# A hybrid decoder layer on one core: the FFN's down-projection by seven block products instead of eight, and its up-projection with the weights as the moving operand

## The chip, the cores and the metric

The kernel runs on one core of a Trainium2 chip. The metric is the device time in microseconds of one execution. Three executions of the kernel before took 1066.48, 1064.62 and 1064.70 us, median 1064.7.

The engines go by these names: PE is TensorE (matrix products), DVE is VectorE, ACT is ScalarE, POOL is GpSimd, SP issues most DMAs.

## The reference: what is computed

One layer over 256 tokens of width 2048, all in float32:

```python
h = rmsnorm(x, g_mix)
z = h @ w_in                       # conv, pooling and attention heads
x = x + concat(conv, pool, att) @ w_out
h = rmsnorm(x, g_ffn)
u = causal_dwconv(h @ w_up, ffn_conv_w) + ffn_conv_b      # width 3 over the tokens
gate, val = split(u, 2)
x = x + (silu(gate) * val) @ w_down
return rmsnorm(x, g_final)
```

`w_up` is 2048 x 11264 and `w_down` 5632 x 2048, so the FFN holds 92.3 and 46.1 of the 202 MB that are read. Each weight is read once and used for 256 tokens.

## The kernel before

**Products.** A float32 operand is split into two float32r parts, `hi` (a rounded copy) and `lo` (the rest), and a product is made of three: hi x hi, hi x lo, lo x hi. Every weight goes through `split_piece`: ACT writes `hi` (L129), DVE subtracts it from the raw tile to give `lo` (L130). The activations are split in the same way when they are made.

**The stream of weights.** All weight tiles, 1 MB each, form one list, `stream`. `next_tile` hands out the next split tile; before it does, it emits the loads up to three tiles ahead (L118, on SP's queue) and the splits up to two ahead. `raw`, `hi` and `lo` have three buffers each.

**The two forms of a product.** `mm_a` (L306, L309) keeps the weights as the stationary operand and streams the activations, 256 tokens of hi and of lo side by side: a matmul of 512 columns with the weight's `hi`, and one of 256 with its `lo`. Its result has channels in the partitions. `mm_b` (L338, L341, L344) keeps 128 tokens of the activation stationary and streams 512 columns of the weights, three matmuls of 512. Its result has tokens in the partitions.

**The FFN.** The up-projection goes by 22 units of 256 gate and 256 value channels, each in form a (`unit_a`). `up_finish` then takes each chunk of 128 channels out of PSUM: `gather` adds the main and the correction columns and multiplies by the row of the norm's factors (ACT L322, DVE L323, L324), ACT applies the last tap and the bias (L747), DVE the other two taps (L751), ACT the silu (L755). The gate times the value is split into `u` (L776 to L778). The units form groups of 8, 7, 5 and 2; `down` multiplies a finished group by `w_down` in form b and adds it to the residual `xt` (`add_in`, L706). It comes after the next group's first unit, that of the last but one group after all units. `down_last` takes the last group by column pieces, with the final norm between them.

**The order.** In the first part and in `down_last`, PE, DVE and ACT keep the program's order. Between them a planner orders each engine's instructions ahead of time, by their place in the program and its own estimate of when their inputs are ready; on the chip each engine then runs its list in that order. Activations lie in three buffers of 32 KB per partition (`apool`), and PSUM gives eight banks of 512 columns.

Of the kernel before, what the change touches and what calls it, by code (L numbers as in the profile page):

```python
# [24 lines left out]
def kernel(  # L25
# [45 lines left out]
    # Per-channel vectors, as columns of 128 channels, by transposing rows of 128.  # L71
# [20 lines left out]
    rows = lambda v: v.rearrange("(r c) -> r c", c=P)  # noqa: E731  # L92
# [10 lines left out]
    stream = []  # (source, nk, ncol, pieces)  # L103
# [4 lines left out]
    def load(i, between=None):  # L108
        src, nk, ncol, pieces = stream[i]
        raw = wpool.tile([P, nk, ncol], F32, tag="raw", name=f"raw_{i}")  # L110
# [23 lines left out]
    def split_tile(i):  # L134
        nk, pieces = stream[i][1], stream[i][3]
        step = nk // pieces
        for j in range(0, nk, step):
            split_piece(i, j, j + step)
        loaded.pop(i)
# [16 lines left out]
    n_units = NF // 2  # L156
    UNITS = [8, 7, n_units - 17, 2]  # sizes of FFN groups in units of 256 channels
# [20 lines left out]
    # The pool's weights: per pair of groups the three chunks' rows, in the columns of  # L178
    # the output chunks that they reach; wp_at[k] is the first of them.
# [17 lines left out]
    # Chunks of the mix in the order in which they come about.  # L197
# [10 lines left out]
    # A group's down-projection comes after the next group's first unit; that of the  # L208
    # last but one after all units.
    sched = []  # L210
    done = 0
    for gi, (a, n) in enumerate(group_of):
        upto = n_units if gi + 2 >= len(group_of) else a + n + 1
        for u in range(done, upto):
            sched.append(("up", u, [g for g, (b, m) in enumerate(group_of) if b <= u][-1]))
        done = upto
        sched.append(("down", gi, None))
    for what, a, b in sched:
        if what == "up" and a == 0:
            for h in (0, 1):  # L220
                plan_a(w_up, 0, (h,))
                plan_a(w_up, D_UP, (h,))
        elif what == "up":
            plan_a(w_up, a * 256)
            plan_a(w_up, D_UP + a * 256)
        else:
            a0, n = group_of[a]
            for n2 in range(2):
                plan_b(w_down, a0 * 2, n * 2, n2 * 1024, 1024, 2)

# [27 lines left out]
    def rstd_of(ssq, nm):  # L258
        """ssq [P, n] sums of squares -> 1 / sqrt(mean + eps), with a Newton step."""
# [14 lines left out]
    def row_of(r, nm):  # L274
        """[P, TB] per-token values -> the same row of S values in every partition."""
# [44 lines left out]
    def gather(ps, row, o, engine=nc.vector):  # L320
        """(main + corrections) * row -> o [P, S] in SBUF."""
        nc.scalar.activation(o, ps[:, S:], AF.Copy)  # L322
        nc.vector.tensor_tensor(o, ps[:, :S], o, op=ALU.add)  # L323
        engine.tensor_tensor(o, o, row, op=ALU.mult)  # L324
# [44 lines left out]
    # The order of the first instructions is that in which the data arrive.  # L369
# [66 lines left out]
    def split_into(o, src, n=S):  # L436
        """float32 [P, n] -> o, its two parts one after the other."""
# [50 lines left out]
    # 1 / (number of tokens averaged) for the first tokens  # L488
# [73 lines left out]
    # The sums run on GpSimd while the next unit's products do; the rest comes after.  # L562
    pending = []

    def pool_sums(ps, i):
# [3 lines left out]
        spans = []  # (first row, last row, group) of this chunk  # L569
# [17 lines left out]
    def pool_means():  # L587
        for i, v, spans, sums in pending:
# [11 lines left out]
            # The convolution's chunks of the mix are free until it comes.  # L600
# [122 lines left out]
    row_2 = None  # L723
    u_tiles = {}

    def up_matmul(u):
        if u:
            return [unit_a(h2T, f"g{u}"), unit_a(h2T, f"v{u}")]
        ps = [[bank(f"pu0_{w}_{mi}") for mi in range(2)] for w in range(2)]
        for h in range(2):  # L730
            for w in range(2):
                mm_a(ps[w], next_tile(), h2T, h * 8, 8, h == 0, h == 1)
                if h == 0 and w == 0:
                    transpose_in(xt, h2T, "g_ffn", range(8, 16), "x2")
        return ps

    def up_finish(ps, u, w):
        """main + corrections, norm, convolution and bias of one half of a unit."""
        outs = []
        for mi in range(2):  # L740
            m = w * NF + u * 2 + mi
            hp = spool.tile([P, S + 2], F32, tag="hpad", name=f"h_{u}_{w}_{mi}", bufs=HPAD)
            nc.gpsimd.memset(hp[:, :2], 0.0)
            gather(ps[mi], row_2, hp[:, 2:])
            t = spool.tile([P, S], F32, tag="w1k", name=f"t_{u}_{w}_{mi}", bufs=6)
            cw = [cvec("ffn_conv_w", j * 2 * NF + m) for j in range(3)]
            nc.scalar.activation(  # L747
                t, hp[:, 2:], AF.Identity, bias=cvec("ffn_conv_b", m), scale=cw[2]
            )
            for s in (1, 0):  # L750
                nc.vector.scalar_tensor_tensor(  # L751
                    t, hp[:, s : s + S], cw[s], t, op0=ALU.mult, op1=ALU.add
# [4 lines left out]
        return outs  # L757

    def up(u, gi):
        nonlocal row_2  # L760
        if gi not in u_tiles:
            u_tiles[gi] = apool.tile([P, 16, 2 * S], F32R, tag="act", name=f"u_{gi}")
        ut = u_tiles[gi]
        base = group_of[gi][0]
        if u == 0:
            ps_g, ps_v = up_matmul(0)
            row_2 = row_of(rstd_sum(ssq4, "x2"), "x2")
            gates = up_finish(ps_g, u, 0)
        else:
            ps_g = unit_a(h2T, f"g{u}")  # L770
            gates = up_finish(ps_g, u, 0)
            ps_v = unit_a(h2T, f"v{u}")
        vals = up_finish(ps_v, u, 1)
        for mi in range(2):
            c = (u - base) * 2 + mi
            nc.vector.tensor_tensor(gates[mi], gates[mi], vals[mi], op=ALU.mult)  # L776
            nc.scalar.activation(ut[:, c, :S], gates[mi], AF.Copy)
            nc.vector.tensor_tensor(  # L778
                ut[:, c, S:], gates[mi], ut[:, c, :S].bitcast(F32), op=ALU.subtract
            )  # L780

    def down(gi):
        ut = u_tiles[gi]
        nk = group_of[gi][1] * 2
        for n2 in range(2):
            ps = [[bank(f"pd_{gi}_{n2}_{tb}_{n}") for n in range(2)] for tb in range(TB)]
            for i in range(nk // 2):
                mm_b(ps, next_tile(), ut, (2 * i, 2 * i + 1), range(TB), i == 0, i == nk // 2 - 1)
            add_in(ps, n2 * 2, range(TB), f"d{gi}")

    # The last group goes by token blocks and column pieces, each followed by its share
    # of the final norm, so that little is left after the last product.
    def down_last(gi):
        ut = u_tiles[gi]
        nk = group_of[gi][1] * 2
# [31 lines left out]
        def partial(tb):  # L827
            """The mean square + eps, but for the last piece."""
# [4 lines left out]
        def rstd_last(tb):  # L833
            """-2 / sqrt(mean square + eps), with a Newton step."""
# [20 lines left out]
        with tc.manual_schedule(engines=IN_ORDER):  # L855
# [32 lines left out]
    for what, a, b in sched:  # L888
        if what == "up":
            up(a, b)  # L890
        elif a < len(group_of) - 1:
            down(a)
        else:
            down_last(a)
# [31 lines left out]
```

## Time and profile before

| | before |
|---|---|
| median of three runs | 1064.7 us |
| the profiled execution: its span | 1064.7 us |
| PE busy | 1054.7 us, 5632 matmuls |
| DVE busy | 703.6 us, 920 instructions |
| ACT busy | 529.0 us, 683 instructions |
| POOL busy | 43.1 us, 163 instructions |
| moved by DMA | 202.01 MB, mean 190 GB/s |

The span goes from the first to the last instruction; the profiled execution's own time is that span. A row of instruction groups gives the line, engine and operation, the output and inputs by their names in the program, the count, then busy time and the mean of one in ns, then the engine's idle time ahead of them and what ended it. "pd" is the down-projection's PSUM, "pa_g" and "pa_v" those of the gate and the value, "pl" that of the last group. Matmuls overlap, so the time of one row is longer than the step from one start to the next. In the view by stretches the columns are the stretch, its length, then PE, weight load, DVE, ACT and POOL busy time with counts, the clock that was granted to PE, and the DMAs' share and rate.

### The profile page before, as it was taken

The numbers are of one execution on the slowest core, as the hardware profiler recorded it, in microseconds if no ns is written. First come the engines' busy times: TensorE is split into PE (matmuls) and PEld (weight loads), VectorE is DVE, ScalarE is ACT, GpSimd is POOL, SyncE is SP. The second block draws the span as 40 slices with busy tenths as digits, with TensorE's granted clock in tenths as the row PEclk, the third lists the DMA queues.
The fourth block names the chain that finished last, engine by engine and source line by source line (L and its number), as shares of the span: only waits on it lengthen the run. The fifth ranks groups of instructions, "written<-read, shape, count | busy, mean of one in ns | idle before, by whom it ended". The sixth has DMA issues, their size and how long they took to land.

```text
span 1064.7 us, 14249 instructions
## 1 busy us (share of the span) xinstructions
PE 1054.7 (99%) x5632; PEld 907.2 (85%) x5632; DVE 703.6 (66%) x920; ACT 529.0 (50%) x683; POOL 43.1 (4%) x163
## 2 busy tenths in 40 slices
PE   9999999999999999999999999999999999999996
PEld 8888898888888888888888888888888888888885
DVE  5677786764556777777744467777754477777655
ACT  5965454443446655555533344554533345555343
POOL 0023500000000000000000000000000000000000
PEclk9999999999999999999999999999999999999998
DMA  9765465455555556555555555655555555654552
GB/s 316 243 224 172 143 206 189 161 195 183 186 185 174 184 196 198 188 181 185 198 198 198 196 171 187 198 185 175 195 198 197 191 174 190 198 177 178 198 198 80
DMA packets 147342, 202.01 MB, mean 190 GB/s; under 512 B 3619, under 2 KB 125771, under 8 KB 147147
## 3 DMA queue, kind: packets, MB, share of 16 engines
q1 hardware_dynamic: 147242, 201.09, 55.8%
q8 instruction: 44, 0.72, 0.3%
q14 instruction: 24, 0.19, 0.0%
q10 hardware_dynamic: 32, 0.01, 0.0%
HBM read 198.99 MB, written 2.10 MB: 189 GB/s over the span
## 4 chain that ended last, share of the span: by engine, by line
PE 98%; DVE 1%; ACT 0%; issue 0%; DVEq 0%
PE pa_v L306 15%; PE pa_g L306 15%; PE pa_g L309 7%; PE pa_v L309 7%; PE pd L338 7%; PE pd L344 7%; PE pd L341 7%; PE po L338 3%; PE po L341 3%; PE po L344 3%; PE pa_cc L306 2%; PE pa_cx L306 2%; PE pa_cb L306 2%; PE pa_pv L306 2%; PE pk L395 2%; PE pa_q L306 1%
## 5 line engine op out<-in xcount | busy, mean ns | idle before, releaser
L130 DVE TENSOR_TENSOR lo<-raw,hi 128x2048 fp32r<-128x2048 f32 (+2 forms) x196 | 425.5, 2172 | 271.6 <-ACT hi L129 270.6
L129 ACT ACTIVATE hi<-raw 128x2048 fp32r<-128x2048 f32 (+2 forms) x196 | 355.9, 1818 | 255.8 <-PE pd L344 98.4
L306 PE MATMUL pa_v<-h2T,hi 128*128 128x512 f32 x672 | 236.7, 396 | 0.0
L306 PE MATMUL pa_g<-h2T,hi 128*128 128x512 f32 x672 | 236.7, 396 | 0.0
L309 PE MATMUL pa_g<-h2T,lo 128*128 128x256 f32 x672 | 188.5, 281 | 0.0
L309 PE MATMUL pa_v<-h2T,lo 128*128 128x256 f32 x672 | 188.5, 281 | 0.0
L306 PEld LDWEIGHTS pa_v<-h2T,hi 128*128 128x128 f32 x672 | 126.0, 188 | 30.0
L306 PEld LDWEIGHTS pa_g<-h2T,hi 128*128 128x128 f32 x672 | 126.0, 188 | 30.0
L309 PEld LDWEIGHTS pa_g<-h2T,lo 128*128 128x128 f32 x672 | 127.0, 189 | 0.1
L309 PEld LDWEIGHTS pa_v<-h2T,lo 128*128 128x128 f32 x672 | 127.0, 189 | 0.0
L338 PE MATMUL pd<-hi,u 128*128 128x512 f32 x320 | 98.6, 389 | 0.0
L341 PE MATMUL pd<-lo,u 128*128 128x512 f32 x320 | 98.5, 389 | 0.0
L344 PE MATMUL pd<-hi,u 128*128 128x512 f32 x320 | 98.5, 389 | 0.0
L751 DVE SCALAR_TENSOR_TENSOR t<-h,cols,t 128x256 f32<-128x256 f32 x176 | 79.1, 480 | 2.2 <-ACT t L747 1.4
L755 ACT ACTIVATE t<-t 128x256 f32<-128x256 f32 x44 | 18.3, 418 | 107.0 <-DVE t L751 107.0
L341 PEld LDWEIGHTS pd<-lo,u 128*128 128x128 f32 x320 | 60.1, 188 | 12.6
L344 PEld LDWEIGHTS pd<-hi,u 128*128 128x128 f32 x320 | 60.1, 188 | 12.4
L338 PEld LDWEIGHTS pd<-hi,u 128*128 128x128 f32 x320 | 59.9, 188 | 12.4
L747 ACT ACTIVATE t<-h,cols 128x256 f32<-128x256 f32 x88 | 49.8, 593 | 0.0
L322 ACT ACTIVATE h<-pa_g 128x256 f32<-128x256 f32 x42 | 16.0, 380 | 61.3 <-PE pa_g L309 61.3
L338 PE MATMUL po<-hi,mixT 128*128 128x512 f32 x128 | 39.6, 391 | 0.0
L341 PE MATMUL po<-lo,mixT 128*128 128x512 f32 x128 | 39.5, 389 | 0.0
(207 smaller groups left out, 1280.9 us busy)
## 6 DMA issues: line engine op xcount, KB each, us to landing
raw<-in_w_up_dram SPq DMA_DIRECT2D x88, 1024.0 KB, 5.0
raw<-in_w_down_dram SPq DMA_DIRECT2D x44, 1024.0 KB, 4.9
raw<-in_w_in_dram SPq DMA_DIRECT2D x28, 1024.0 KB, 4.9
raw<-in_w_out_dram SPq DMA_DIRECT2D x16, 1024.0 KB, 4.9
raw<-in_w_kv_dram SPq DMA_DIRECT2D x4, 1024.0 KB, 5.2
raw<-in_w_kv_dram SPq DMA_DIRECT2D x6, 512.0 KB, 8.3
memt<-in_mem_dram SPq DMA_DIRECT2D x8, 256.0 KB, 7.7
xt<-in_x_dram SPq DMA_DIRECT2D x4, 512.0 KB, 6.7
```

The costliest lines, as they stand in the source:

```text
L129: nc.scalar.activation(hi[:, s, :], raw[:, s, :], AF.Copy)
L130: nc.vector.tensor_tensor(lo[:, s, :], raw[:, s, :], hi[:, s, :].bitcast(F32), op=ALU.subtract)
L306: nc.tensor.matmul(ps[mi], hi[:, kk, c], actT[:, k, :], start=first and kk == 0, stop=False)
L309: nc.tensor.matmul(ps[mi][:, S:], lo[:, kk, c], actT[:, k, :S], start=False, stop=last and kk == nk - 1,)
L322: nc.scalar.activation(o, ps[:, S:], AF.Copy)
L338: nc.tensor.matmul(ps[tb][n], ah, hi[:, kk, c], start=f, stop=False)
L341: nc.tensor.matmul(ps[tb][n], ah, lo[:, kk, c], start=False, stop=False)
L344: nc.tensor.matmul(ps[tb][n], al, hi[:, kk, c], start=False, stop=l)
L395: nc.tensor.matmul(psk[mi], wt[0][:, j, c], mT[:, k, :], start=k == 0, stop=False)
L747: nc.scalar.activation(t, hp[:, 2:], AF.Identity, bias=cvec("ffn_conv_b", m), scale=cw[2])
L751: nc.vector.scalar_tensor_tensor(t, hp[:, s : s + S], cw[s], t, op0=ALU.mult, op1=ALU.add)
L755: nc.scalar.activation(t, t, AF.Silu)
```

## The change

Three things change in the FFN; what comes before it stays.

**The up-projection goes in form b.** The 11 units now have 512 gate and 512 value channels. A tile is 512 rows x 512 columns of `w_up`; for each of two token blocks it takes 4 x 3 matmuls of 512 columns (`up`). After four tiles the result, tokens in the partitions, is copied out of PSUM by ACT with the norm's factor as scale (`z`), and `up_finish` turns it back with eight PE transposes of 128 x 128 in the middle of the next tile (`todo`). The taps then read PSUM directly; `gather` and its multiplication are gone here, and so are POOL's clearings of the margin.

**The down-projection of all groups but the last goes by 2 x 2 blocks.** A group is now 1024 channels (the last one 512). Its activations are cut into two token blocks and the even and odd chunks of channels; a half of `w_down`'s columns (`p`) into the same channels and two column pieces of 512. `turn` makes the seven left operands from differences and sums of the four blocks and splits them. On the right, `Blocks` keeps three raw buffers and forms the operands in place: `b11` becomes `b11 + b12`, then `+ b22` (both on DVE, `add`), later `+ b21`, and `b12` becomes `b12 + b22` (both by a DMA that POOL issues and that adds its source, read from `w_down` in DRAM, to what lies in the target, `add_far`). Seven products of 12 matmuls each (`prod`) accumulate in three PSUM chains, and after each product DVE adds the chain's state to or subtracts it from one quarter of `xt`. The second half of the last but one group is done in the plain way, with four blocks and 24 matmuls for each (`plain`). The blocks' loads are issued from the splits of the half before.

**The order of the program.** A group's products stand between the next group's up tiles: none after the first three, one after each of the next twelve, two after the last. In the last group, which has eight tiles, they come as 0, 0, 0, 1, 1, 1, 2, 6. `sums` and `ffn` (the raw product of gate and value, and the three block buffers) take two of the three large activation buffers; the last group's `u` lies in the front of `h2T`.

The core of the diff:

```diff
-    UNITS = [8, 7, n_units - 17, 2]  # sizes of FFN groups in units of 256 channels
+    n_units = NF // 4
+    UNITS = [2] * (n_units // 2) + [1]
...
+    N_PROD = 7
+    class Blocks:
...
+        def load(self, name):
+            nc.sync.dma_start(self.buf(name), self.source(name))
+        def add_far(self, to, what):
+            nc.gpsimd.dma_start(self.buf(to), self.source(what), accum_op=ALU.add)
+        def add(self, to, what):
+            nc.vector.tensor_tensor(self.buf(to), self.buf(to), self.buf(what), op=ALU.add)
+        def split(self, i, idx):
+            raw = self.buf(("b11", "b11", "b11", "b12", "b22", "b21", "b11")[idx])
...
+            nc.scalar.activation(hi, raw, AF.Copy)
+            nc.vector.tensor_tensor(lo, raw, hi.bitcast(F32), op=ALU.subtract)
+            if idx == 0:
+                self.add("b11", "b12")
+                self.add_far("b12", "b22")
+            elif idx == 1:
+                self.add("b11", "b22")
+            elif idx == 3:
+                self.load("b21")
+                self.add_far("b11", "b21")
+            elif self.next is not None and idx >= 4:
...
+                self.next.load(names[idx - 4])
...
+        elif n == 2:
+            after = [0, 0, 0] + [1] * 12 + [2]
+        else:
+            after = [0, 0, 0, 1, 1, 1, 2, 6]
...
+    def up(u, b):
...
+        for tb in range(TB):
+            for kk in range(4):
+                k = 4 * q + kk
+                ah = h2T[:, k, tb * P : (tb + 1) * P]
+                al = h2T[:, k, S + tb * P : S + (tb + 1) * P]
+                for n, (x_, y_) in enumerate(((ah, hi), (ah, lo), (al, hi))):
+                    nc.tensor.matmul(
+                        ps[tb], x_, y_[:, kk, :],
+                        start=k == 0 and n == 0, stop=k == KC - 1 and n == 2,
+                    )
+            if tb == 0 and todo:
+                todo.pop(0)()
...
+            nc.scalar.activation(z[tb], ps[tb], AF.Copy, scale=r_2[0][:, tb : tb + 1])
...
     def up_finish(u, w, z):
...
+                nc.tensor.transpose(pt[-1][:, o : o + P], z[tb][:, c * P : (c + 1) * P], ident)
...
+    def turn(gi):
...
+        tt(t[:, 0], a21, a22, op=ALU.subtract)
+        tt(t[:, 2], a11, a21, op=ALU.subtract)
+        tt(t[:, 1], t[:, 0], a11, op=ALU.subtract)
...
+        tt(t[:, 3], t[:, 1], a12, op=ALU.add)
+        nc.scalar.activation(sums[:, 1:5, 0], t, AF.Copy)
...
+        tt(sums[:, 1:5, 1], t, sums[:, 1:5, 0].bitcast(F32), op=ALU.subtract)
...
+    def prod(bl, i):
+        hi, lo = next_tile()
+        chain, first, tb, right, op = (
+            ("a", True, 0, 0, ALU.add),
+            ("b", True, 1, 1, ALU.add),
+            ("a", False, 0, 1, ALU.subtract),
+            ("a", False, 1, 1, ALU.subtract),
+            ("b", False, 0, 1, ALU.add),
+            ("c", True, 0, 0, ALU.add),
+            ("a", False, 1, 0, ALU.add),
+        )[i]
...
+        for j in range(4):
+            ah, al = sums[:, i, 0, j, :], sums[:, i, 1, j, :]
+            for n, (a, b) in enumerate(((ah, hi), (ah, lo), (al, hi))):
+                nc.tensor.matmul(
+                    ps, a, b[:, j, :], start=first and j == 0 and n == 0,
+                    stop=j == 3 and n == 2, skip_group_check=True,
+                )
...
+        nc.vector.tensor_tensor(o, o, ps, op=op)
```

More of the change, by code (lines that the diff above doesn't have):

```diff
@@ L153, in next_tile @@
         return split.pop(i)
-    n_units = NF // 2
-    UNITS = [8, 7, n_units - 17, 2]
+    n_units = NF // 4
+    UNITS = [2] * (n_units // 2) + [1]
+    assert sum(UNITS) == n_units and NF % 4 == 0
     D_UP = DFF
@@ new lines, with buf, split @@
+    class Plain(Blocks):
+        ORDER = ("b11", "b21", "b12", "b22")
+        def buf(self, name):
+            return rawd[(self.seq + self.ORDER.index(name)) % 3]
+        def split(self, i, idx):
+            raw = self.buf(self.ORDER[idx])
+            hi, lo = split[i] = [
+                wpool.tile([P, 4, 512], F32R, tag=t, name=f"{t}_{i}") for t in ("hi", "lo")
+            ]
+            nc.scalar.activation(hi, raw, AF.Copy)
+            nc.vector.tensor_tensor(lo, raw, hi.bitcast(F32), op=ALU.subtract)
+            if idx == 0:
+                self.load("b22")
@@ L210, with part_of @@
+    blocks = []
+    for gi in range(len(group_of) - 1):
+        for p in range(2):
+            kind = Plain if gi == len(group_of) - 2 and p == 1 else Blocks
+            blocks.append(kind(len(blocks), gi, p))
+            if len(blocks) > 1:
+                blocks[-2].next = blocks[-1]
+    def part_of(u, b):
+        return (b // 2 % 2, b % 2 + b // 4 * 2) if u == 0 else (b // 4, b % 4)
     sched = []
-    done = 0
+    prods = []
     for gi, (a, n) in enumerate(group_of):
[L213 to L217, printed above, removed]
@@ L218 @@
-    for what, a, b in sched:
[L219 to L225, printed above, removed]
-        else:
-            a0, n = group_of[a]
-            for n2 in range(2):
-                plan_b(w_down, a0 * 2, n * 2, n2 * 1024, 1024, 2)
+        n_t = 8 * n
+        if not prods:
+            after = [0] * n_t
+        elif n == 2:
+            after = [0, 0, 0] + [1] * 12 + [2]
+        else:
+            after = [0, 0, 0, 1, 1, 1, 2, 6]
@@ new lines @@
+        assert sum(after) == len(prods)
+        for t in range(n_t):
+            sched.append(("up", a + t // 8, t % 8))
+            for _ in range(after[t]):
+                sched.append(prods.pop(0))
+        if gi < len(group_of) - 1:
+            prods = []
+            for b in blocks[2 * gi : 2 * gi + 2]:
+                n = len(b.ORDER) if isinstance(b, Plain) else N_PROD
+                prods += [("plain" if isinstance(b, Plain) else "prod", b, i) for i in range(n)]
+    for what, a, b in sched:
+        if what == "up":
+            w, q = part_of(a, b)
+            plan_b(w_up, 4 * q, 4, w * D_UP + a * 512, 512, 4)
+        else:
+            stream.append((a, None, b, 1))
@@ L232, in turn_pair @@
+    a0, n = group_of[-1]
+    for n2 in range(2):
+        plan_b(w_down, a0 * 4, n * 4, n2 * 1024, 1024, 2)
     def turn_pair(xt, k, nm):
@@ L737, in up_finish @@
-    def up_finish(ps, u, w):
-        outs = []
[L740 to L745, printed above, removed]
+    sums = apool.tile([P, N_PROD + 1, 2, 4, P], F32R, tag="act", name="sums")
+    ffn = apool.tile([P, 4, 2048], F32, tag="act", name="ffn")
@@ new lines @@
+    u_raw = ffn[:, 0, :].rearrange("p (c t) -> p c t", t=S)
+    rawd = [ffn[:, 1 + i, :].rearrange("p (j c) -> p j c", c=512) for i in range(3)]
+    for name in ("b11", "b22", "b12"):
+        blocks[0].load(name)
+    u_last = h2T[:, : 4 * UNITS[-1], :]
+    up_ps, up_gates, todo, r_2 = {}, {}, [], []
+    def up(u, b):
+        w, q = part_of(u, b)
+        if q == 0:
+            up_ps[w] = [bank(f"pu{u}_{w}_{tb}") for tb in range(TB)]
+        ps = up_ps[w]
+        hi, lo = next_tile()
[11 more added lines that the diff above has]
+                todo.pop(0)()
+        if u == 0 and b == 0:
+            for k in range(8, 16, 2):
+                split_turned(turn_pair(xt, k, "x2"), h2T, "g_ffn", k)
+            r_2.append(rstd_sum(ssq4, "x2"))
+        if q < 3:
+            return
+        z = []
+        for tb in range(TB):
+            z.append(spool.tile([P, 512], F32, tag="w2k", name=f"z_{u}_{w}_{tb}"))
+            nc.scalar.activation(z[tb], ps[tb], AF.Copy, scale=r_2[0][:, tb : tb + 1])
+        todo.append(lambda: up_finish(u, w, z))
@@ new lines, in up_finish @@
+    def up_finish(u, w, z):
+        pt = []
+        for c in range(4):
+            if c % 2 == 0:
+                pt.append(bank(f"pz{u}_{w}_{c}"))
+            for tb in range(TB):
+                o = c % 2 * S + tb * P
+                nc.tensor.transpose(pt[-1][:, o : o + P], z[tb][:, c * P : (c + 1) * P], ident)
+        outs = []
+        for c in range(4):
+            v = pt[c // 2][:, c % 2 * S : (c % 2 + 1) * S]
+            m = w * NF + u * 4 + c
+            tag, n, bufs = ("w1k", S, 6) if w else ("hpad", PAD + S, HPAD)
+            t = spool.tile([P, n], F32, tag=tag, name=f"t_{u}_{w}_{c}", bufs=bufs)[:, :S]
@@ L756, in up_finish @@
             outs.append(t)
[L757 to L789, printed above, removed]
+        if w == 0:
+            up_gates[u] = outs
+            return
+        gates = up_gates.pop(u)
+        gi = [g for g, (a, n) in enumerate(group_of) if a <= u][-1]
@@ new lines, in up_finish @@
+        for c in range(4):
+            if gi < len(group_of) - 1:
+                o = u_raw[:, (u - group_of[gi][0]) * 4 + c, :]
+                nc.vector.tensor_tensor(o, gates[c], outs[c], op=ALU.mult)
+            else:
+                nc.vector.tensor_tensor(gates[c], gates[c], outs[c], op=ALU.mult)
+                split_into(u_last[:, c, :], gates[c])
+        if gi < len(group_of) - 1 and u == group_of[gi][0] + group_of[gi][1] - 1:
+            turn(gi)
+    def turn(gi):
+        v = u_raw.rearrange("p (j s) (b t) -> p s b j t", s=2, b=TB)
+        a11, a12, a21, a22 = v[:, 0, 0], v[:, 1, 0], v[:, 0, 1], v[:, 1, 1]
+        t = wpool.tile([P, 4, 4, P], F32, tag="raw", name=f"turn_{gi}")
+        tt = nc.vector.tensor_tensor
+        parts = [(0, a11), (5, a12), (6, a22)]
+        if gi == len(group_of) - 2:
+            parts.append((7, a21))
+        for at, src in parts:
+            nc.scalar.activation(sums[:, at, 0], src, AF.Copy)
+        tt(t[:, 0], a21, a22, op=ALU.subtract)
+        tt(t[:, 2], a11, a21, op=ALU.subtract)
+        tt(t[:, 1], t[:, 0], a11, op=ALU.subtract)
+        for at, src in parts[:1]:
+            tt(sums[:, at, 1], src, sums[:, at, 0].bitcast(F32), op=ALU.subtract)
+        tt(t[:, 3], t[:, 1], a12, op=ALU.add)
+        nc.scalar.activation(sums[:, 1:5, 0], t, AF.Copy)
+        for at, src in parts[1:]:
+            tt(sums[:, at, 1], src, sums[:, at, 0].bitcast(F32), op=ALU.subtract)
+        tt(sums[:, 1:5, 1], t, sums[:, 1:5, 0].bitcast(F32), op=ALU.subtract)
@@ new lines, in plain @@
+    def plain(bl, i):
+        hi, lo = next_tile()
+        right, odd = divmod(i, 2)
+        if odd == 0:
+            chains["plain"] = [bank(f"pp_{bl.seq}_{i}_{tb}") for tb in range(TB)]
+        for tb in range(TB):
+            ps = chains["plain"][tb]
+            at = ((0, 7), (5, 6))[odd][tb]
+            for j in range(4):
+                ah, al = sums[:, at, 0, j, :], sums[:, at, 1, j, :]
+                for n, (a, b) in enumerate(((ah, hi), (ah, lo), (al, hi))):
+                    nc.tensor.matmul(
+                        ps, a, b[:, j, :], start=odd == 0 and j == 0 and n == 0,
+                        stop=odd == 1 and j == 3 and n == 2,
+                    )
+            if tb == 0 and todo:
+                todo.pop(0)()
+            if odd:
+                c0 = bl.p * 1024 + right * 512
+                o = xt[:, tb, c0 : c0 + 512]
+                nc.vector.tensor_tensor(o, o, ps, op=ALU.add)
@@ L888 @@
     for what, a, b in sched:
[L889 to L894, printed above, removed]
+        {"up": up, "prod": prod, "plain": plain}[what](a, b)
+    down_last(len(group_of) - 1)
 _INS = [
```

52 lines of the change are left out of this document (33 added, 19 removed).

## The prediction

> **What bounds the kernel now.** I read the page's busy shares first, then its chain of waits, then TensorE's (PE's) own waits, then the busy time by stretch.
>
> ```profile
> span 1064.7 us, 14249 instructions
> ...
> PE 1054.7 (99%) x5632; PEld 907.2 (85%) x5632; DVE 703.6 (66%) x920; ACT 529.0 (50%) x683; POOL 43.1 (4%) x163
> ...
> PE 98%; DVE 1%; ACT 0%; issue 0%; DVEq 0%
> ```
> ```profile
> PE warm L67 <- DVE ones L58: 1.0, 1, 1.0
> PE pk L395 <- DVE mT L249: 0.3, 1, 0.3
> ```
> ```profile
> 325.60:1040.00 714.40, 714.40 (x3794) 613.77 (x3793) 477.05 (x601) 347.28 (x406) 9.01 (x86) 1.00 0.56 189
> 1040.00:1064.70 24.70, 15.98 (x94) 14.00 (x92) 14.96 (x31) 9.24 (x25) 0.00 (x0) 0.88 0.23 86
> ```
>
> The waits view holds these two PE waits and no others, 1.3 us in all; the chain is 98% PE. In the FFN (second row group: span, then PE, weight load, VectorE, ScalarE, GpSimd, clock, DMA share, GB/s) PE is busy for every microsecond at clock 1.00, while VectorE (DVE) works 477 of 714 us (67%), ScalarE (ACT) 347 (49%). So a PE instruction fewer is worth its full step, as long as nothing else makes PE wait. The span equals the median of the three timed runs (1064.7), so nothing is added around it.
>
> **PE, step by step.** A matmul's row lasts longer than its step because neighbours overlap, so I take steps from starts, in the timeline, and the chain's piece for transposes:
>
> ```profile
> 400.07 0.39 PE L306 MATMUL pa_v<-h2T,hi 128*128 128x512 f32 x1
> ...
> 411.17 0.39 PE L306 MATMUL pa_g<-h2T,hi 128*128 128x512 f32 x1
> ```
> ```profile
> 560.22 0.62 PE L338 MATMUL pd<-hi,u 128*128 128x512 f32 x2
> ...
> 569.74 0.62 PE L338 MATMUL pd<-hi,u 128*128 128x512 f32 x2
> ```
> ```profile
> 326.15 1.75 PE pt_x L237 x16
> ```
> ```profile
> L237 PE MATMUL pt_x<-ident,xt 128*128 128x128 f32 x64 | 8.8, 273 | 0.0
> ```
>
> Between 400.07 and 411.17 lie 32 pairs (512 columns, then 256): 0.3469 us a pair. Between 560.22 and 569.74 lie 42 matmuls of 512: 0.2267 us each. Sixteen transposes take 1.75 us: 0.109 each.
>
> Up-projection: 22 units x 2 halves x 2 chunks x 16 = 1408 pairs now, 488.4 us. After, 88 tiles of 24 matmuls = 2112, 478.8 us: -9.6. The same columns flow; only the short matmuls' extra goes.
>
> Down-projection of the first five groups: 40 chunks x 2 token blocks x 4 column pieces x 3 = 960 matmuls now; after, nine halves of 7 x 12 and one plain half of 4 x 24 = 852. 108 fewer: -24.5.
>
> Added: the up-projection now comes out with tokens in the partitions, so it is turned back: 22 x 8 = 176 transposes, +19.2. Removed: two transposes of the norm's row, -0.2.
>
> Sum: -9.6 - 24.5 + 19.2 - 0.2 = -15.1, so 1049.6 us if PE still never waits. The transposes' shape and type stand in the trace, so I take 0.109; the row's mean of 0.273 is the other end. The Trainium skill ("TensorE: Matmul & The Clock Gate", Part 4: PE-mode transpose) speaks against this part: it gives about 275 ns for a transpose in a kernel and says that the fast clock does not engage for transposes. By that figure 176 would cost 48.4 us and the sum would be 1078.8; the trace's sixteen in a row at 0.109 contradict it as a spacing, and it survives only as a row's latency.
>
> **VectorE and ScalarE.** What these gain and lose, by the rows that keep shapes apart (last pair: busy us, mean ns):
>
> ```profile
> L130 DVE TENSOR_TENSOR lo<-raw,hi 128x2048 fp32r<-128x2048 f32 x175 | 401.4, 2294 | 264.8 <-ACT hi L129 264.5
> L751 DVE SCALAR_TENSOR_TENSOR t<-h,cols,t 128x256 f32<-128x256 f32 x176 | 79.1, 480 | 2.2 <-ACT t L747 1.4
> L324 DVE TENSOR_TENSOR h<-h,row_x 128x256 f32<-128x256 f32 x88 | 35.4, 421 | 0.8
> L776 DVE TENSOR_TENSOR t<-t,t 128x256 f32<-128x256 f32 x44 | 16.8, 420 | 0.0
> L706 DVE TENSOR_TENSOR xt<-pd,xt 128x512 f32<-128x512 f32 x24 | 14.9, 683 | 0.0
> ```
> ```profile
> L129 ACT ACTIVATE hi<-raw 128x2048 fp32r<-128x2048 f32 x175 | 335.2, 1915 | 255.8 <-PE pd L344 98.4 <-issue 84.2 <-PE po L344 39.2
> L747 ACT ACTIVATE t<-h,cols 128x256 f32<-128x256 f32 x88 | 49.8, 593 | 0.0
> L755 ACT ACTIVATE t<-t 128x256 f32<-128x256 f32 x44 | 18.3, 418 | 107.0 <-DVE t L751 107.0
> L479 ACT ACTIVATE misc<-pv,r_mem 128x512 fp32r<-128x512 f32 x2 | 1.3, 675 | 0.0
> ```
>
> DVE work of one full group of 1024 channels after: 16 up tiles and 14 product blocks to subtract, 30 x 2.294 = 68.8; four local block sums of the same size, 9.2; 14 additions out of PSUM, 9.6; 32 convolution steps, 15.4; 8 gate products, 3.4; the turn into the seven left operands, 4 + 3 operations of 512 and one of 2048, 7.1. Together 113.5 us. The gather's two operations per chunk (L323, L324) are gone. PE's group is 552 x 0.2267 + 32 x 0.109 = 128.6 us, so DVE would be 88% busy. ACT: 30 x 1.915, 8 copies out of PSUM at 0.675, 16 x 0.593, 8 x 0.418 and 3.7 of the turn = 79 us, 61%.
>
> The average fits; the order decides. A weight tile needs ACT, then DVE, 4.2 us, and there are three buffers each of `hi` and `lo`, so work can start only two tiles ahead (ACT's wait on `pd L344` above is that buffer). An up tile is 24 matmuls, 5.44 us, a product 2.72. A split may begin two items before its use, 8.16 us, and so stands a delay of 3.9 us. Plain windows ask 2 x 2.29 + 0.68 = 5.3 us of DVE in 8.16. Where a unit is finished, 8 convolution steps (3.8) or these and four products (5.5) come on top, and after each of the first two products of a half a local sum of 2.29.
>
> The tightest places, by setting these in order by hand: at the turn (rest of the finish 5.5, turn 7.1, five splits 11.5 and two additions 1.4, 25.5 us of DVE against four tiles and a product, 25.3 with the transposes) the split of the fourth tile ends just when PE wants it; then product 2, whose split waits for both sums while the gate half is finished, ends within 0.1 us of its time. I charge 1 us to each of the five turns, since the hand-offs between engines are not in my rows. Lower end 0, upper end in the rivals.
>
> **DMA.** Local sum on DVE apart, each of nine halves has two 1 MB additions issued by GpSimd (POOL) that the trace does not show at all. The nearest rows are plain loads of the same size, and the rate that the DMAs have reached:
>
> ```profile
> raw<-in_w_down_dram SPq DMA_DIRECT2D x44, 1024.0 KB, 4.9
> ```
> ```profile
> DMA to landing us min/median/max: 4.0/4.9/8.5
> ```
> ```profile
> DMA  9765465455555556555555555655555555654552
> GB/s 316 243 224 172 143 206 189 161 195 183 186 185 174 184 196 198 188 181 185 198 198 198 196 171 187 198 185 175 195 198 197 191 174 190 198 177 178 198 198 80
> ```
>
> Such an addition reads both its addend and its target: lower bound one landing, 4.9 us, upper bound two of the longest, 17. The first (into `b12`) may start when the sum into `b11` has read `b12`, some 3.8 us into product 0, and product 3's split must begin 4.2 us before product 3, three tile-and-product windows (24.5 us) after product 0: 16.5 us. So all but the upper end is hidden behind products 0 to 2; I take two median landings, 9.8 us, no cost. The second (into `b11`, after product 2's split, for product 6) has a window more. Behind a late one stands ACT's in-order queue, with all later splits, and so PE. POOL's queue is otherwise empty (9.0 us in 714, the memsets that go). Traffic rises to 1 + 6/7 blocks of 1.05 MB per 8.16 us = 239 GB/s, under the 316 of the first slice; the loads that a block adds to SP's queue wait for splits as the weight loads already do.
>
> **The ends.** At the FFN's start three block loads (14.7 us of landings) wait for `mixT` and may stand before up tiles; at the end the last unit's finish (7.2 us of DVE) falls among the four plain products (21.8 us). I charge 1 us together, from 0 to 8 (one and a half tiles). The last rows are otherwise unchanged.
>
> Forecast: 1049.6 + 5 + 1 = 1056, rounded.
>
> **Rivals.** *DVE becomes the bound in the windows that have a finish.* For it: 88%, and waits cannot be worked ahead of. Against it: 3 us are free in each plain window. If nothing is carried over, a group loses 11.4 - 9.0 twice (finish, sum, two splits, one addition against 8.16 + 0.87) and 10.8 - 9.0 once, 6.6 us; four groups, 26: 1076. It decides the sign from 3.8 us a group on.
>
> *The first DMA addition lands late.* For it: nothing in the trace bounds it. At four plain landings, 20 us, product 3 waits 3.1 us in nine halves, 28: with the 6 above 1084; each further microsecond costs 9. It turns the gain into a loss from about 17.5 us on. The Trainium skill ("SBUF — State Buffer", Who interferes with whom) says that a DVE instruction with two SBUF inputs blocks a GpSimd instruction that reads SBUF; no run here shows whether that touches the issue of such an addition.
>
> *Transposes step at their row's mean*, 0.273: 48.0 instead of 19.2, 1078 without stalls. The sixteen in 1.75 us speak against it.
>
> *The ends cost their 8 us and the turns 2 each*, 1049.6 + 8 + 10 less what overlaps, about 1065: no change.
>
> **How the numbers follow.** Forecast case 0.55, with a range of its own of 1048 to 1062. DVE bound 0.17 (1060 to 1085), late additions 0.15 (1065 upward), transposes 0.03, ends 0.10. Range 1047 to 1082: below it nothing but a mis-sized step, above it about half of the late additions. A difference under 0.2% (2.1 us) can't be told from none. Faster: 0.53 of the forecast case, 0.03 of DVE bound, 0.04 of the ends, 0.60; same 0.08; slower 0.32.
>
> **What would show it.** Right: up matmuls at 0.227 us, 852 products, 176 transposes near 0.11, DVE near 590 us in the FFN, PE waits of a few us, on `lo` at the turns. Wrong: PE waiting on `lo` by tens of us in every group (DVE), ACT `hi` waiting for a DMA into the block buffers (additions), or transposes spaced by 0.27.

## The result and the profile after

The changed kernel takes 1046.4 us, median of four runs (1046.35 to 1048.0), against 1064.7 before: a ratio of 0.983 (95% interval 0.9816 to 0.9844), 18.3 us or 1.7% faster. The forecast was 8.7 us faster, so the gain is twice as large, and the time lies 0.6 us below the range.

The page of the changed kernel, its span and busy times:

```profile
span 1044.2 us, 12615 instructions
...
PE 1033.6 (99%) x4994; PEld 868.2 (83%) x4994; DVE 781.3 (75%) x833; ACT 587.0 (56%) x646; POOL 57.5 (6%) x93
```

PE's waits (total, times, longest) are these, and no others:

```profile
PE warm L67 <- DVE ones L58: 1.1, 1, 1.1
PE pk L492 <- DVE mT L346: 0.8, 1, 0.8
```

Both lie in the first 10 us. PE lost 21.1 us of busy time and 638 matmuls, DVE gained 77.7 us and ACT 58.0, and PE still waits for nobody. The FFN runs from the first up matmul to the first of `pl`. The timeline before, then after:

```profile
320.34 0.39 PE L306 MATMUL pu<-h2T,hi 128*128 128x512 f32 x1
...
1033.73 0.62 PE L338 MATMUL pl<-hi,u 128*128 128x512 f32 x2
```
```profile
318.58 0.39 PE L844 MATMUL pu<-hi,h2T 128*128 128x512 f32 x1
...
1013.28 0.62 PE L435 MATMUL pl<-hi,h2T 128*128 128x512 f32 x2
```

That is 713.4 and 694.7 us: 18.7 of the 20.5 us between the two spans. The other 1.8 arise before the FFN, in code that didn't change. Timeline, before and after:

```profile
6.78 2.04 PE L395 MATMUL pk<-mT,hi 128*128 128x512 f32 x4 [0.26 <-DVE mT L249]
```
```profile
6.79 1.17 PE L492 MATMUL pk<-mT,hi 128*128 128x512 f32 x4 [0.85 <-DVE mT L346]
```

The same four matmuls took 2.04 us in one execution and 1.17 in the other, and more of this kind follows in the next microseconds. In the traces' records of the granted clock, full speed begins 10.6 us after the start in the one and 5.2 us in the other; until then these matmuls step at about twice the time (0.43 us against 0.23). The profiled execution of before was its 1066.48 us one, 1.8 over the span and over the median alike. So its own time is not its span, and the forecast's line that nothing lies around the span was a misreading; the sum, made against 1064.7, was not moved by it.

The chain of waits after, over a plain tile and one with transposes, with a start, a length and what ran:

```profile
442.15 2.72 PE pp_b L946 x12
444.87 5.44 PE pu L844 x24
...
469.35 2.73 PE pu L844 x12
472.07 0.87 PE pz L870 x8
472.95 2.77 PE pu L844 x12
```

A product is 12 x 0.2267 us, a plain tile 24 x 0.2267. Eight transposes take 0.87, but the matmuls around them slow down a little too: this tile takes 6.37, 0.93 more than a plain one. By the starts, the 21 tiles that hold eight take 0.96 more on average. Now the FFN's terms, from starts and these steps:

| term | predicted | measured | from |
|---|---|---|---|
| up-projection | -9.6 | -15.0 | before 493.8, the FFN less the other rows and `pt_x` (1.75); after 478.8, 2112 at 0.2267 |
| down-projection, 960 to 852 matmuls | -24.5 | -24.5 | 217.6, then 193.1 at 0.2267 |
| transposes | +19.2 | +21.1 | the FFN after, less the other rows and `pt_x`; 22 x 0.96 by the tiles |
| row transposes | -0.2 | -0.2 | not measured apart |
| stalls at the turns, the ends | +6 | 0 | no PE wait in the FFN |
| sum | -9.1 | -18.7 | the FFN; the medians -18.3 |

Three terms were off: the up-projection by -5.4 us, the transposes by +1.9, the stalls by -6. The first is a remainder in this table; the pairs below give it independently. The experiments go to the first and the last.

### The profile page after: what moved, and what is told of

Same layout as the page of the kernel before. It is cut to its first block, busy times and chain, and to the rows that moved or that the text cites. A ratio compares the mean times of both kernels' runs of the same rounds, so it can differ in the third digit from the quotient of the medians.

```text
span 1044.2 us, 12615 instructions
## 1 busy us (share of the span) xinstructions
PE 1033.6 (99%) x4994; PEld 868.2 (83%) x4994; DVE 781.3 (75%) x833; ACT 587.0 (56%) x646; POOL 57.5 (6%) x93
## 4 chain that ended last, share of the span: by engine, by line
PE 98%; DVE 1%; ACT 0%; issue 0%; DVEq 0%
PE pu L844 46%; PE pp_a L946 9%; PE pp_b L946 5%; PE po L441 3%; PE po L438 3%; PE po L435 3%; PE pp_c L946 2%; PE pa_cc L403 2%; PE pa_cx L403 2%; PE pa_cb L403 2%; PE pa_pv L403 2%; PE pp L965 2%; PE pz L870 2%; PE pa_q L403 1%; PE pk L492 1%; PE pa_pv L406 1%
## 5 line engine op out<-in xcount | busy, mean ns | idle before, releaser
L844 PE MATMUL pu<-hi,h2T 128*128 128x512 f32 x1408 | 448.9, 391 | 0.0
L132 DVE TENSOR_TENSOR lo<-raw,hi 128x2048 fp32r<-128x2048 f32 (+3 forms) x156 | 333.2, 2137 | 129.7 <-ACT hi L131 128.8
L131 ACT ACTIVATE hi<-raw 128x2048 fp32r<-128x2048 f32 (+3 forms) x156 | 279.4, 1794 | 120.2 <-PE po L441 39.3
L844 PEld LDWEIGHTS pu<-hi,h2T 128*128 128x128 f32 x1408 | 264.4, 188 | 54.5
L844 PE MATMUL pu<-lo,h2T 128*128 128x512 f32 x704 | 274.3, 390 | 0.0
L253 DVE TENSOR_TENSOR lo<-ffn,hi 128x2048 fp32r<-128x2048 f32 x63 | 144.3, 2290 | 66.8 <-ACT hi L252 66.8
L252 ACT ACTIVATE hi<-ffn 128x2048 fp32r<-128x2048 f32 x63 | 120.6, 1916 | 98.3 <-PE pu L844 73.8
L844 PEld LDWEIGHTS pu<-lo,h2T 128*128 128x128 f32 x704 | 132.3, 188 | 27.3 <-DVE lo L132 0.7
L946 PE MATMUL pp_a<-hi,sums 128*128 128x512 f32 x288 | 94.5, 389 | 0.0
L880 DVE SCALAR_TENSOR_TENSOR t<-pz,cols,t 128x255 f32<-128x255 f32 (+1 forms) x176 | 79.6, 478 | 10.2 <-ACT t L878 9.2
L878 ACT ACTIVATE t<-pz,cols 128x256 f32<-128x256 f32 x88 | 46.9, 557 | 46.2 <-DVE t L880 24.1
L242 POOL DMA_DIRECT2D ffn<-in_w_down_dram x18 | 23.2, 1291 | 615.4 <-DVE ffn L245 494.4
L859 ACT ACTIVATE z<-pu,r_x 128x512 f32<-128x512 f32 x44 | 30.1, 686 | 46.4 <-PE pu L844 46.4
## 6 DMA issues: line engine op xcount, KB each, us to landing
ffn<-in_w_down_dram POOLq DMA_DIRECT2D x18, 1024.0 KB, 10.4
```

The lines of the kernel that those rows point to most:

```text
L131: nc.scalar.activation(hi[:, s, :], raw[:, s, :], AF.Copy)
L132: nc.vector.tensor_tensor(lo[:, s, :], raw[:, s, :], hi[:, s, :].bitcast(F32), op=ALU.subtract)
L252: nc.scalar.activation(hi, raw, AF.Copy)
L253: nc.vector.tensor_tensor(lo, raw, hi.bitcast(F32), op=ALU.subtract)
L844: nc.tensor.matmul(ps[tb], x_, y_[:, kk, :], start=k == 0 and n == 0, stop=k == KC - 1 and n == 2,)
L878: nc.scalar.activation(t, v, AF.Identity, bias=cvec("ffn_conv_b", m), scale=cw[2])
```

## The experiments

### What a pair costs in the kernel before

Three stretches of before that hold up-projection alone, PE's busy time with counts second:

```profile
331.69:522.10 190.41, 190.41 (x1101) 167.89 (x1100) 143.25 (x207) 103.07 (x137) 3.30 (x33) 1.00 0.57 188
609.18:767.46 158.28, 158.28 (x897) 137.18 (x896) 114.03 (x159) 81.45 (x106) 2.61 (x26) 1.00 0.56 187
843.65:979.32 135.67, 135.67 (x769) 117.69 (x768) 97.32 (x135) 69.50 (x90) 1.81 (x18) 1.00 0.56 187
```

The first holds 549 pairs, 0.3468 us each, the second 448 and the third 384, 0.3533 each, with the same instructions, clock 1.00 and no wait. The stretch that the forecast read was in the first. So 832 of the 1408 pairs run at the longer step, 5.4 us in all, and 576 x 0.3468 + 832 x 0.3533 = 493.7, the table's 493.8. First test: two extra transposes between two pairs of the units 9 and 16.

```diff
-    def mm_a(ps, wt, actT, k0, nk, first, last):
+    def mm_a(ps, wt, actT, k0, nk, first, last, extra=0):
...
+                if extra and kk == 1 and mi == 0:
+                    pe_ = bank(f"extra_{extra}")
+                    for e in range(2):
+                        nc.tensor.transpose(pe_[:, e * P : (e + 1) * P], ident, ident)
```

> The kernel before, with two transposes of the identity into a spare bank in the first tile of units 9 and 16; nothing else. In the trace of before the pair of 512 and 256 columns steps at 0.3468 us from the row's transposes at 331.6 to the first down-projection at 522, and at 0.3533 in all units behind it. Theory A (the step depends on what came before, and two transposes in a tile set it back): the 832 pairs of units 9 to 21 go at 0.3468, 832 x 0.0065 = 5.4 us less, 0.4 us more for four transposes: 1059.7. Theory B (it depends on the buffers or banks that these units use): still 0.3533, 1065.1.

Measured: 1065.2 us, ratio 1.0006 (0.9998 to 1.0015), and the timeline gives 0.3533 still (the second row is 33 pairs on):

```profile
899.62 0.40 PE L310 MATMUL pa_v<-h2T,hi 128*128 128x512 f32 x1
...
911.28 0.40 PE L310 MATMUL pa_g<-h2T,hi 128*128 128x512 f32 x1
```

A break there does nothing. The next two put it elsewhere: the same two transposes inside a pair, between its 512 and its 256 columns, and sixteen between the first two tiles of each of the two units.

```diff
                     ps[mi], hi[:, kk, c], actT[:, k, :], start=first and kk == 0, stop=False
                 )
+                if extra and kk == 1 and mi == 0:
+                    pe_ = bank("extra")
+                    for e in range(2):
+                        nc.tensor.transpose(pe_[:, e * P : (e + 1) * P], ident, ident)
```

> The kernel before, with two transposes of the identity in the first tile of units 9 and 16, this time inside a pair, between its 512 and its 256 columns, where the transposes of the norm's row stood in the pooling units and the pair went on at 0.347. Theory A (the short step is a state that such a break sets): units 9 to 21 at 0.3468, 5 us less: 1059.7. Theory B (the units' buffers or banks): 0.3533 stays, 1065.1.

```diff
             mm_a(ps, next_tile(), actT, h * 8, 8, h == 0, h == 1)
+            if nm in ("g9", "g16") and h == 0:
+                pe_ = bank("extra")
+                for e in range(16):
+                    c = slice(e % 4 * P, (e % 4 + 1) * P)
+                    nc.tensor.transpose(pe_[:, c], ident, ident)
```

> The kernel before, with sixteen transposes of the identity between the first two tiles of units 9 and 16, as those of x stood in unit 0, behind which the pair went from 0.3533 to 0.3468. Theory A (a state that such a break sets): 5.4 us less for the pairs, 3.5 us more for 32 transposes: 1062.8. Theory B: 0.3533 stays, 1068.2.

Inside a pair: 1062.6 us, ratio 0.9976 (0.9966 to 0.9985). Unit 9's break changed nothing, unit 16's brought the short step (33 pairs between the first two rows, 34 between the last two):

```profile
659.74 0.40 PE L306 MATMUL pa_g<-h2T,hi 128*128 128x512 f32 x1
671.39 0.40 PE L306 MATMUL pa_v<-h2T,hi 128*128 128x512 f32 x1
...
899.70 0.39 PE L306 MATMUL pa_v<-h2T,hi 128*128 128x512 f32 x1
911.49 0.39 PE L306 MATMUL pa_g<-h2T,hi 128*128 128x512 f32 x1
```

Sixteen between tiles: 1062.9 us, ratio 0.9982 (0.9973 to 0.9992), and both breaks brought it (34 pairs):

```profile
639.76 0.40 PE L306 MATMUL pa_g<-h2T,hi 128*128 128x512 f32 x1
...
651.55 0.40 PE L306 MATMUL pa_v<-h2T,hi 128*128 128x512 f32 x1
```

The sum agrees: 832 x 0.0065 = 5.4 us saved, 32 transposes at 0.109 = 3.5 spent, 1.9 net, and 1.9 was measured. Inside a pair, what unit 16 and those behind it should save, 384 x 0.0065 less four transposes, is 2.1 us; 2.2 was measured, between the two theories. So the pair's step is a state that lasts over hundreds of matmuls and that a break can set back; it does not belong to the units' buffers or banks. Which break does so, and why, stays open. For the change it means that form a cost 493.8 us, not 488.4.

### What the seven products are worth

The changed kernel with every half of the down-projection in the plain way, so form b of the up-projection alone:

```diff
-            kind = Plain if gi == len(group_of) - 2 and p == 1 else Blocks
+            kind = Plain
...
-            after = [0, 0, 0] + [1] * 12 + [2]
+            after = [0, 0, 0] + [1, 0, 1, 1, 0, 1, 0, 1, 1, 0, 1, 1, 0]
...
-            after = [0, 0, 0, 1, 1, 1, 2, 6]
+            after = [0, 0, 0, 1, 0, 1, 1, 5]
```

> The kernel after, with all ten halves of the down-projection done the plain way: eight block products, no sums of blocks, up-projection still in form b. Theory A (only PE's steps count): 108 matmuls of 0.2267 come back, 24.5 us: 1070.9. Theory B (the seven products cost hidden time in ACT, DVE and DMA work, which is now gone): less than that, 1066 to 1069.

Measured: 1069.9 us, ratio 1.0047 (1.0033 to 1.006), no PE wait in the FFN.

```profile
PE 1057.4 (99%) x5102; PEld 888.2 (83%) x5102; DVE 673.8 (63%) x765; ACT 537.5 (50%) x623; POOL 34.3 (3%) x75
```

108 matmuls more than after cost 23.5 us: the seven products are worth what the count says, to within 1 us (24.5 predicted). Form b alone costs 5.2 us: by the measured terms -15.0 + 21.1 - 0.2 = +5.9, by the forecast's +9.4.

### How late a DMA addition may land

In the changed kernel, the view of line 242, the DMA issues on POOL's queue (18, of 1 MB each):

```profile
DMA to landing us min/median/max: 9.7/10.4/12.2
```

The addition takes 10.4 us (9.8 had been taken), at most 12.2, inside the 16.5 us that the forecast found. To see the edge, each addition was issued twice, the second behind the first (the addend counts twice, so the right operands differ):

```diff
             nc.gpsimd.dma_start(self.buf(to), self.source(what), accum_op=ALU.add)
+            nc.gpsimd.dma_start(self.buf(to), self.source(what), accum_op=ALU.add)
```

> The kernel after, with each DMA addition issued twice, the second after the first: b22 and b21 come in twice, so the right operands of products 3 and 6 are others than the reference needs; the work on PE, ACT and DVE is the same. A landing was 10.4 us in the median, so the pair takes about 21. Theory A (16.5 us of room for the first addition, as in the prediction): product 3 waits some 4 us in nine halves: 1082. Theory B (there is more room than that): 1046 to 1050.

Measured: 1093.2 us in one execution, above both theories. The chain, then PE's waits:

```profile
568.11 10.46 DMA ffn<-in_w_down_dram
...
578.86 12.46 DMA ffn<-in_w_down_dram
```
```profile
PE pp_a L947 <- DVE xt L953: 13.4, 9, 3.6
PE pp_a L947 <- ACT hi L253: 8.4, 3, 4.2
PE pp_a L947 <- DVE lo L254: 8.0, 5, 1.8
```

This pair lands 23.2 us after its first start. The nine waits on `xt` come at product 3, one in each half, 13.4 us or 1.5 each: the addition to `xt` stands behind product 3's late split in DVE's order. So the first addition had some 21 us from its issue, more than the 16.5 worked out. The other eight waits (16.4 us) come at product 6, behind the second pair, in the four second halves and in the last one; there the second pair is issued while the first is still under way and takes some 30 us. The mechanism of the rival is real; a single addition of 10.4 us is far from it. The whole loss, 46.9 us of span, is more than the 29.8 of these waits; the other 17.2 are PE busy time (1050.8 against 1033.6). The mean clock fell from 0.998 to 0.986, which is worth some 13 us of 1091 (more on that below); the remaining 4 are not explained.

### What the additions by DMA save

The two sums on DVE instead, as the first two are done:

```diff
-                self.add_far("b12", "b22")
+                self.add("b12", "b22")
...
-                self.add_far("b11", "b21")
+                self.add("b11", "b21")
```

> The kernel after, with the two DMA additions of each half replaced by additions on DVE of the blocks that lie in the buffers. DVE then has 113.5 + 9.2 = 122.7 us of work in a group of 128.6. Theory A (DVE is at the edge where a group turns, and two of four further additions fall near it): 2 us at each turn and some at the finishes, 1056. Theory B (the order leaves room): 1046 to 1049.

Measured: 1052.0 us, ratio 0.9882 (0.9867 to 0.9898), 5.6 us above the changed kernel, between the theories. The waits for `lo`, of the weight load and of the matmul:

```profile
PEld pu L844 <- DVE lo L132: 6.9, 5, 1.7
PE pu L844 <- DVE lo L132: 4.7, 5, 1.2
```

Of the five waits of the matmul, four come at the first four turns (0.5 to 1.2 us each). The fifth (0.9) comes in the last group, where one of the added sums stood for a load, and a wait of 0.2 for `hi` comes there too. All eighteen additions went to DVE (818.9 us, 78%), and in the full groups only those at the turns are seen. So it is not DVE's average that binds.

### How much room the turn has

The last subtraction of `turn` (128 x 2048) done twice, and four times, for DVE time with no other effect:

```diff
         tt(sums[:, 1:5, 1], t, sums[:, 1:5, 0].bitcast(F32), op=ALU.subtract)
+        tt(sums[:, 1:5, 1], t, sums[:, 1:5, 0].bitcast(F32), op=ALU.subtract)
```

> The kernel after, with the last subtraction of the turn (128 x 2048, 2.29 us of DVE) done twice; the result is unchanged. Theory A (at the turn DVE's work ends just when PE wants it, as the order by hand had it): each of five turns waits 2.3 us more: 1057. Theory B (some us of room): 1046.5.

> The same with that subtraction done four times, 6.9 us more at each turn. Theory A: 5 x 6.9 = 34 more, 1081. Theory B (some us of room at each turn): the excess over the room, 1047 to 1065; together with the run with one more, the room is read off.

Once more: 1048.0 us (two runs, ratio 0.984, 0.9819 to 0.9861), 1.6 us above the changed kernel. PE itself waits once, at the fifth turn; the weight load's other three waits are 0.2 us each:

```profile
PE pu L844 <- DVE lo L132: 1.2, 1, 1.2
PEld pu L844 <- DVE lo L132: 2.3, 4, 1.6
```

Three times more: 1077.7 us (two runs, ratio 1.0118, 1.0086 to 1.0151), between the theories, now with a wait of product 1 on the delayed operand:

```profile
PE pp_b L949 <- DVE sums L927: 16.0, 5, 3.9
...
PE pp_a L949 <- ACT hi L252: 1.7, 1, 1.7
PE pu L844 <- DVE lo L132: 1.5, 2, 1.2
```

At the four full turns the wait is 3.6 to 3.9 us for 6.6 us of further work (three times 2.20, the distance of starts), so product 1's operands have nearly 3 us of room there, not the zero of the hand count. That room lies behind the tight split: at these turns the order puts the further subtractions after the split of the tile behind product 0 (DVE, 563.00 and then 565.21, in the kernel with one more). At the fifth turn it stands ahead of that split, and the room is 1 us. The waits sum to 19.2 us, yet the span is 29.5 us longer (1073.7). One turn by stretches (the last three columns are the granted clock, the DMAs' share and GB/s):

```profile
576.00:580.00 4.00, 1.66 (x8) 1.04 (x6) 4.00 (x3) 0.56 (x1) 0.00 (x0) 1.00 0.30 117
...
582.00:586.00 4.00, 4.00 (x10) 3.09 (x10) 4.00 (x4) 0.00 (x0) 0.00 (x0) 0.50 0.83 266
586.00:588.00 2.00, 2.00 (x7) 1.62 (x6) 1.91 (x3) 1.69 (x1) 0.78 (x1) 0.61 1.04 383
```

Behind the 3.9 us wait the clock is at 0.50 and stays low for some 6 us; at full clock four microseconds hold 18 matmuls, here 10. All four waits of 3.6 to 3.9 us are followed by such a stretch, in two cases a shorter one; the shorter waits of the fifth turn (up to 1.7 us) by none. PE's busy time grew by 10.0 us (1043.6), and that with the waits is the loss. The Trainium skill ("TensorE: Matmul & The Clock Gate", Part 1: The HAM clock gate) says that the clock halves after an idle window of about 3.4 us; these rows agree. In the kernel with doubled additions the clock also fell to 0.50 in the course of two waits of 2.1 and 1.8 us with a single matmul between them (they end at 677.9 and 680.2 us), so the idle time need not be in one piece. Once, in the first version of the next section, it was at 0.50 from 453.8 us on for some 3 us, behind waits of only 0.3 and 1.3 us; why stays open. The waits of at most 1.2 us in the two lighter kernels (one more subtraction, sums on DVE) left the mean clock at 0.997, that of the kernel before.

### Whether form b was needed

The up-projection back in form a with seven products, its factor multiplied by GpSimd. In the first version `turn` stands ahead of the previous group's last two products, which so read the next group's left operands:

```diff
-        hi, lo = next_tile()
-        for tb in range(TB):
...
+        mm_a(ps, next_tile(), h2T, h * 8, 8, h == 0, h == 1)
...
+            gather(ps[mi], r_2[0], v, nc.gpsimd)
```

> The kernel after, with the up-projection back in form a (weights stationary, pairs of 512 and 256 columns, no transposes back), the seven products as they are; the norm's factor is multiplied in by GpSimd (128 x 256, 0.74 us in the trace of before) instead of DVE. PE by its steps: 1064.7 - 24.5 = 1040.2, less if the pairs step at 0.3468 throughout. DVE has 113.5 + 6.7 = 120 us in a group of 127. Theory A (only PE's steps count): 1036 to 1042. Theory B (DVE, now with three operations to a chunk, binds at turns and finishes): over 1046.

Measured: 1099.6 us, ratio 1.0323 (1.0305 to 1.0341), with four waits of nearly 10 us:

```profile
PE pp_c L923 <- ACT sums L891: 38.4, 4, 9.9
```

This tells of the order, not of form a. In the second version the turn comes after the next group's first tile:

```diff
+        if todo:
+            todo.pop(0)()
...
-            turn(gi)
+            todo.append(lambda: turn(gi))
```

> The up-projection in form a with seven products again, with the turn put where the kernel after has it, behind the next group's first tile, so that it no longer comes ahead of the last two products of the group before, which read what it overwrites. PE by its steps: 756 + 96 products at 0.2267 and 1408 pairs at 0.3533, which is their step wherever products stood between them in the run before: 1043.8. Theory A (only PE's steps count): 1043 to 1046. Theory B (DVE with its third operation to a chunk, and GpSimd's multiplication in the chain of the turn, bind): 5 to 15 more, 1049 to 1059.

Measured: 1066.8 us, ratio 1.0015 (1.0005 to 1.0025), above both theories. PE is busy for 1035.1 us, only 1.5 more than in the changed kernel, but the span of the profiled execution is 18.5 us longer (1062.7), with waits in many places:

```profile
PE pp_a L925 <- ACT hi L252: 10.0, 5, 2.2
PE pu L405 <- DVE lo L132: 6.8, 9, 1.4
```

DVE is at 827.7 us, 46.4 more than in the changed kernel, most of it the additions of `gather`:

```profile
L419 DVE TENSOR_TENSOR z<-pu,z 128x256 f32<-128x256 f32 x88 | 36.1, 419 | 28.1 <-ACT z L418 27.8
```

So in the two orders that were run the seven products don't pay with form a. Form b, which by itself costs 5.2 us, takes `gather` from DVE, and beside it they run without a wait. That DVE's load and the multiplication on GpSimd cause the loss is argued from these rows; how much each gives isn't separated. No version was faster than the changed kernel.

## Why the prediction was right in sign and too small

**What bounds, the counts and most steps: right.** PE bounds both kernels; 852 matmuls of products, 2112 up matmuls at 0.2267 and the down-projection's -24.5 came as worked out (23.5 when undone). The transposes, whose two prices lay furthest apart, step at 0.109:

```profile
L870 PE MATMUL pz<-ident,z 128*128 128x128 f32 x176 | 23.5, 272 | 0.0
```

The row's 272 ns is again a duration; eight take 0.87 us in the chain. What the forecast left out is that they break a tile: with the slower matmuls around them they cost 21.1 us, not 19.2. The rival fell, and with it the 48.4 us, an estimate by the 275 ns that the Trainium skill ("TensorE: Matmul & The Clock Gate", Part 4: PE-mode transpose) gives. Nor do the traces bear out that the fast clock does not engage for transposes: the four of `pt_mem` at 9.47 us in before, where the clock is not yet up, take 1.05 us, those at 8.27 us in after 0.60.

**The step that failed first: "Between 400.07 and 411.17 lie 32 pairs ... 0.3469 us a pair".** The number was right for that stretch and was taken for all 1408. A second stretch, after 609, would have shown 0.3533. The term was -15.0, not -9.6.

**The step that failed second: "I charge 1 us to each of the five turns", and 1 us for the ends.** The 6 us were 0: PE waits nowhere in the FFN. The turn was set in order with the means of DVE's rows as if they were steps, the very thing that was avoided on PE. The timeline at a turn of the changed kernel:

```profile
548.06 2.29 DVE L132 TENSOR_TENSOR lo<-raw,hi 128x2048 fp32r<-128x2048 f32 x1
550.26 0.48 DVE L880 SCALAR_TENSOR_TENSOR t<-pz,cols,t 128x255 f32<-128x255 f32 x1
550.65 0.69 DVE L916 TENSOR_TENSOR turn<-ffn 128x512 f32<-128x512 f32 x1
551.25 0.48 DVE L880 SCALAR_TENSOR_TENSOR t<-pz,cols,t 128x254 f32<-128x254 f32 x1
```

Starts lie 2.20, 0.39 and 0.60 us apart where the durations are 2.29, 0.48 and 0.69: neighbours overlap by 0.09 us. The forecast's 25.5 us held about 27 instructions (12 of the finish, 8 of the turn, 5 splits, 2 additions), so up to 2.4 us less, about the size of the room that the experiments found. That the one makes up the other is argued; no run shows it apart from the order of the instructions. The overlap shows in a whole group too:

```profile
561.89:690.90 129.01, 129.01 (x585) 106.93 (x585) 106.98 (x97) 76.01 (x67) 5.10 (x5) 1.00 0.78 228
```

The group takes 129.0 us (128.6 predicted), but DVE is busy for 107.0, not 113.5: 83%, not 88%. In the whole FFN it is 555 us, where the forecast looked for 590. The split that was to end just when PE wants it does so:

```profile
562.71 2.29 DVE L132 TENSOR_TENSOR lo<-raw,hi 128x2048 fp32r<-128x2048 f32 x1
...
564.45 0.40 PE L844 MATMUL pu<-hi,h2T 128*128 128x512 f32 x1
564.68 0.38 PE L870 MATMUL pz<-ident,z 128*128 128x128 f32 x2
565.06 0.50 PE L844 MATMUL pu<-lo,h2T 128*128 128x512 f32 x1
```

The tight place was thus found where it is (the tile behind the first product): DVE writes `lo` until 565.00, and two of the eight transposes, which the order puts here, fill PE's 0.38 us until then. They had to be done anyway, so nothing is lost.

**The range.** "Below it nothing but a mis-sized step" was the case that came: the pair's step and the stalls were mis-sized in the same direction, and the transposes' 1.9 us took back only a part.

**The rivals.** DVE did not become the bound; 2.2 us more at the turns begin to cost. The additions landed in time, in half of the room. What the forecast lacked in its price of a late one was the clock: every wait of 3.6 us or more, and some shorter ones close together, were followed by several microseconds at half clock. The ends cost nothing that a PE wait shows.

## What to carry to other kernels

Take an instruction's step from the distance of starts on every engine, not only on PE, and at several stretches of the run; a row's mean counts the overlap with its neighbour again at each instruction. When a change moves work from a full engine to one with room, the fullest moment decides rather than the average: here a turn had 1 to 3 us left while DVE was 83% busy. A form that costs PE time by itself may still be the right partner if it frees the engine that the other half of the change fills.

## What the runs showed of the hardware

Unexpected were two things. Pairs of a 512 and a 256 column matmul step by 0.3468 or by 0.3533 us for hundreds of matmuls, and some breaks of the pattern switch them back. And DVE and GpSimd slow each other where a multiplication of GpSimd runs beside one of DVE's large operations. In the kernel with form a and the late turn, the group of product splits, which takes 2290 ns on average in the changed kernel, and one of them with the multiplication beside it:

```profile
L253 DVE TENSOR_TENSOR lo<-ffn,hi 128x2048 fp32r<-128x2048 f32 x63 | 149.6, 2375 | 28.0 <-ACT hi L252 28.0
```
```profile
559.38 2.72 DVE L253 TENSOR_TENSOR lo<-ffn,hi 128x2048 fp32r<-128x2048 f32 x1
559.90 2.79 POOL L420 TENSOR_TENSOR z<-z,row_x 128x256 f32<-128x256 f32 x1
```

Of the 63, the 14 that a multiplication overlaps take 2.67 us on average, the other 49 2.29. Of the 88 multiplications, 16 take 2.6 to 2.8 us, the others 0.7 to 0.9. The Trainium skill ("SBUF — State Buffer", Who interferes with whom) says that the two engines share a port pair; these rows agree.
